# A hybrid encoder block on one core: the front stages in another order, the softmax normalised in one multiplication per token tile

## The chip, the cores and the metric

One NeuronCore of a Trainium2 chip runs the whole program: 1 launch, inputs and output in device memory. The metric is the device time of one execution in microseconds (us). The program before takes a median of 1157.8 us over three runs.

## The reference

One layer on 256 tokens of 1024 features, in float32. What is computed, cut to its lines:

```python
proj = jnp.einsum('bsd,de->bse', x, w_in[l])
(qa, ckv, qi, ki, wi, qb, kb, vb, ga, gb) = jnp.split(proj, split_at, axis=-1)
...
y_a = sparse_indexed_attention(qa, ckv, qi, ki, wi, w_uk[l], w_uv[l])
y_b = chunk_band_attention(qb, kb, vb, rel_bias[l])
merged = (jax.nn.sigmoid(ga) * (y_a @ w_branch_a[l])
          + jax.nn.sigmoid(gb) * (y_b @ w_branch_b[l]))
x = layer_norm(DN_ALPHA * x + merged @ w_out[l], ln1_g[l], ln1_b[l])
ffn = moe_ffn(x, ...)          # top 4 of 32 experts, clamped SwiGLU
x = layer_norm(DN_ALPHA * x + ffn, ln2_g[l], ln2_b[l])
```

Branch A selects 64 keys for each query with an indexer and attends to them; branch B attends to its chunk and those before it, with a bias. Both end in a softmax over keys for 8 heads.

## The kernel before, in words

The program has two parts. The **front** computes everything up to the router; the **experts** follow, 32 of them, each with 12 MB of weights.

SBUF is cut into 25 slots of 1 MB (`NSLOT`). Every weight is a chunk of one slot. SP, the queue that issues the loads, takes chunks in one fixed list (`plan`): first the front's 24 chunks (16 of `w_in`, 2 of each branch matrix, 4 of `w_out`), then the experts' chunks in the order of use. A load is issued when a slot is free; how many slots it must leave free after each chunk's use is the table `RESERVE` (`pump`). So the loads of the experts' weights begin while the front still runs, as far as its slots allow. Up to the first expert 23 of their chunks are issued.

The front's products run on exact halves. `ahead` splits chunk after chunk: ScalarE (ACT) rounds it to `hi`, in two instructions of 128x1024 (L175), and GpSimd (POOL) or VectorE (DVE) subtracts to get `lo`, again in two (L180). The table `LO_ENGINE` says which engine subtracts for each of the 24 chunks, `AHEAD` how many chunks ahead this is done.

TensorE (PE) follows the order in which the body is written. `project_T(g)` is group g of the input projections (two chunks, 96 matmuls of 256 columns, three for each pair of blocks: hi by hi, lo by hi, hi by lo; feature-major), `project(g)` the same token-major. `head_scores` makes the scores of one token tile; its sink adds scale and bias on DVE (L419). `exps` takes the maximum (DVE, L406) and then 16 exponentials per branch on ACT (L408) that also give the sums. `normalise` (L411 to L414) divides: 16 instructions per branch, one per head and token tile. `attend` turns the probabilities with 24 transposes on PE (L454), copies them to SBUF, and takes the weighted sum of the values (L464). `branch` (L511) multiplies with the branch matrix.

The order before, on PE: groups 0, 1, index scores, group 2, scores of B, group 3 (the values of B), scores of A, group 4 (gate), attend B, group 5 (gate), attend A, groups 6 and 7 (gate), branch A, branch B, output projection (`wo`), norm, router, and the first expert.

Of the kernel before, what the change touches and what calls it, by code (L numbers as in the profile page):

```python
# [48 lines left out]
def body(nc, tc, slots, sm, psp, xT_d, x_d, w_g0, w_qi, w_in, ikgb_d, wuk_d,  # L49
# [4 lines left out]
    # ---------------------------------------------------------------- slots and loads  # L54
# [42 lines left out]
    for i in range(2):  # L97
        plan(("ba", i), wba_d[i])
        plan(("bb", i), wbb_d[i])
# [27 lines left out]
    # ---------------------------------------------------------------- first loads  # L127
# [13 lines left out]
    # ---------------------------------------------------------------- constants and small loads  # L141
# [28 lines left out]
    # ---------------------------------------------------------------- exact halves of float32 operands  # L170
# [12 lines left out]
    order = [("in", i) for i in range(16)] + [("ba", 0), ("ba", 1), ("bb", 0), ("bb", 1)] + [("wo", i) for i in range(4)]  # L183
    IN, BA, BB, WO = 0, 16, 18, 20
    halves = []

    def ahead(n):
        """splits the first n chunks of that order"""
# [66 lines left out]
    def project(g, sink):  # L255
        """group g of the input projections, token-major"""
# [13 lines left out]
    def project_T(g, sink):  # L270
        """group g of the input projections, feature-major; two row blocks share a bank, so only the first starts it"""
# [21 lines left out]
    # k_idx layer norm and c_kv rms norm, token-major  # L293
# [26 lines left out]
    def head_scores(qT, kT, tb, sink):  # L320
        """pairs of heads lie on the two halves of the partitions"""
# [14 lines left out]
    # ---------------------------------------------------------------- B queries and keys, the indexer  # L336
# [51 lines left out]
    # ---------------------------------------------------------------- A queries  # L388
# [11 lines left out]
    V.memset(sB[1][0:64, :, 192:256], NEG)  # L400

# [3 lines left out]
    def exps(s, w, tb):  # L405
        V.tensor_reduce(mx[:, w, tb, :], s[tb], axis=AX.X, op=ALU.max, negate=True)  # L406
        for h in range(H):
            A.activation(s[tb][:, h, :], s[tb][:, h, :], AF.Exp, bias=mx[:, w, tb, h:h + 1],  # L408
                         accum_out=sums[:, w, tb, h:h + 1])

    def normalise(s, w, tb):  # L411
        V.reciprocal(sums[:, w, tb, :], sums[:, w, tb, :])
        for h in range(H):
            V.tensor_scalar(s[tb][:, h, :], s[tb][:, h, :], sums[:, w, tb, h:h + 1], None, op0=ALU.mult)  # L414
# [7 lines left out]
    for tb in range(NT):  # L422
        head_scores(qbT, lambda j: kbT[:, j, :], tb, score_sink(sB))
        exps(sB, 1, tb)
    free(1)
    sa0_s = slot("sa0_vb")
    sa1_s = slot("sa1")
    sA = [sa0_s[:, 0:1024].rearrange("p (h s) -> p h s", h=8), sa1_s.rearrange("p (h s) -> p h s", h=8)]
    for tb in range(NT):
        sl = slice(KOFF[tb], KOFF[tb] + KEYS[tb])  # L430
        for h in range(H):
            V.scalar_tensor_tensor(sA[tb][:, h, :], negd[:, sl], 2.0 ** -(h + 1), amask[:, sl],
                                   op0=ALU.mult, op1=ALU.add)
    free(1)
    vb = sa0_s[:, 1024:2048].rearrange("p (b c) -> p b c", b=2)
    project(3, lambda tb, p: acopy(vb[:, tb, :], p))
    normalise(sB, 1, 0)
    normalise(sB, 1, 1)
    for tb in range(NT):
        head_scores(qaT, lambda j: kaT[:, j, :], tb, score_sink(sA))  # L440
        exps(sA, 0, tb)
    free(2)

    y_s = [slot("yA"), slot("yB")]
    yHL = [[t[:, o:o + 1024].rearrange("p (j t) -> p j t", j=4) for o in (0, 1024)] for t in y_s]

    def attend(s, v, w):
        pts = [slot("pt0"), slot("pt1")]
        pT = [t[:, 0:1536].rearrange("p (b h t) -> p b h t", b=3, h=4) for t in pts]
        for j2 in range(2):  # L450
            for bi, (tb, sb) in enumerate(((0, 0), (1, 0), (1, 1))):
# [3 lines left out]
                (vcopy if bi != 1 else acopy)(pT[j2][:, bi, :, :].rearrange("p h t -> p (h t)"), p)  # L455
        for j2 in range(2):
            o = bank("pv")
            for jj in range(2):
                for tb in range(NT):
                    for sb in range(tb + 1):  # L460
                        for par in range(2):
# [3 lines left out]
                                      v[:, sb, h * 64:(h + 1) * 64], pT[j2][:, tb + sb, i, :],  # L465
                                      start=(sb == 0), stop=(sb == tb), skip_group_check=True)
            hi, lo = [t[:, 2 * j2:2 * j2 + 2, :] for t in yHL[w]]
# [3 lines left out]
    sg_s = [slot("sgA"), slot("sgB")]  # L471
    sg = [s.rearrange("p (k t) -> p k t", k=KD) for s in sg_s]

    def gate_sink(w, n):
        return lambda js, p: A.activation(sg[w][:, 4 * n + js.start:4 * n + js.stop, :], p, AF.Sigmoid)

    project_T(4, gate_sink(0, 0))
    attend(sB, vb, 1)
    free(2)
    normalise(sA, 0, 0)  # L480
    normalise(sA, 0, 1)
    project_T(5, gate_sink(0, 1))
    attend(sA, va, 0)
    free(3)
# [5 lines left out]
    mg = sg[1]  # L490
# [18 lines left out]
    yHL = [[t.bitcast(F32R) for t in hl] for hl in yHL]  # L509

    def branch(w, c, ps):  # L511
        """chunk c of a branch's rows; at the last one the gate and, for B, the sum of the two and its halves"""
        for f in range(KD):
# [10 lines left out]
            if w:  # L524
# [5 lines left out]
    for c in range(2):  # L530
        ahead(BA + c + 1 + AHEAD[BA + c])
        branch(0, c, ps)
# [5 lines left out]
    for c in range(2):  # L538
        ahead(BB + c + 1 + AHEAD[BB + c])
        branch(1, c, ps)  # L540
# [8 lines left out]
    def norm_apply(tb, groups):  # L549
        """z = (x1 - mean) * rstd, and x1 = z * g + b"""  # L550
# [38 lines left out]
    def route_sums(copy=vcopy):  # L589
        """the router's products by experts, in four sums over two row blocks each"""  # L590
# [7 lines left out]
    def route(tb):  # L598
        """the router's logits (the norm's gain in the weights, its offset in the row), and which experts a token takes"""
# [9 lines left out]
    def count_up(tb):  # L609
        """the place of each token among an expert's tokens; far off for the tokens that it doesn't take"""  # L610
# [51 lines left out]
    # the second token tile's last columns in two halves, for a shorter way from their sums to the norm  # L662
# [66 lines left out]
    # ---------------------------------------------------------------- experts  # L729
# [9 lines left out]
    def combine_weights(pt, gated):  # L739
        """pt = the gated one-hot rows turned, from their two halves of 64 columns for each token tile"""  # L740
# [6 lines left out]
    def dispatch_weights(g):  # L747
        """for the pair g of experts"""
# [39 lines left out]
    def down(hT, wd):  # L788
        """the halves of the columns on the halves of the partitions"""
# [7 lines left out]
    def rows_of(e, p, first=0, size=512):  # L797
        """an expert's rows to its half of the pair's partitions"""
# [4 lines left out]
    def combine(g):  # L803
        """adds a pair's rows to the sums"""
# [90 lines left out]
    def down_biases():  # L895
        """the gates' share of the down biases; the largest count of an expert's tokens"""
# [62 lines left out]
    # the last expert: the sums move to PSUM  # L959
# [14 lines left out]
    # ---------------------------------------------------------------- last expert's end, second norm  # L974
# [111 lines left out]
```

## Time and profile before

| | us |
|---|---|
| three runs | 1158.95, 1157.16, 1157.80 |
| median | 1157.8 |
| span of the profiled execution, first to last instruction | 1156.1 |
| first matmul of the first expert, from the span's start | 221.0 |

The profile comes from one more execution of the same program. It gives that execution's span; what lies around the span isn't in it. The lowest of the three runs is 1.1 us above the span and the median 1.7 us. Busy shares over the span: PE 92%, DVE 30%, ACT 20%, POOL 7%; the DMA engines moved 437.5 MB, 378 GB/s on average. The page's slices are 28.9 us wide; the first eight hold the front.

### The profile page before, as it was taken

The numbers are of one execution on the slowest core, as the hardware profiler recorded it, in microseconds if no ns is written. First come the engines' busy times: TensorE is split into PE (matmuls) and PEld (weight loads), VectorE is DVE, ScalarE is ACT, GpSimd is POOL, SyncE is SP. The second block draws the span as 40 slices with busy tenths as digits, with TensorE's granted clock in tenths as the row PEclk, the third lists the DMA queues.
The fourth block names the chain that finished last, engine by engine and source line by source line (L and its number), as shares of the span: only waits on it lengthen the run. The fifth ranks groups of instructions, "written<-read, shape, count | busy, mean of one in ns | idle before, by whom it ended". The sixth has DMA issues, their size and how long they took to land. (4 is left out here: it accounts for less than half of the span.)

```text
span 1156.1 us, 13824 instructions
## 1 busy us (share of the span) xinstructions
PE 1067.6 (92%) x5599; PEld 540.9 (47%) x5599; DVE 351.9 (30%) x811; ACT 227.6 (20%) x424; POOL 85.5 (7%) x60
## 2 busy tenths in 40 slices
PE   8997899999899999999899999996699999999896
PEld 8987899634244443434343434341243434343432
DVE  6797826412212322121212121210212121212124
ACT  3645342221011111111111111110011111111112
POOL 4113723000000000000000000001000000000001
PEclk9997999999899999999999999998799999999998
DMA  8940747999999999999999999999989999999995
GB/s 335 382 154 1 280 180 306 359 420 422 407 405 421 421 420 421 421 421 421 421 421 421 421 422 421 421 422 422 418 353 421 421 421 421 421 421 421 421 421 189
DMA packets 63932, 437.51 MB, mean 378 GB/s; under 512 B 7252, under 2 KB 7892, under 8 KB 11892
## 3 DMA queue, kind: packets, MB, share of 16 engines
q1 hardware_dynamic: 61270, 421.61, 88.5%
q0 software_dynamic: 1728, 12.58, 2.6%
q10 hardware_dynamic: 864, 2.36, 0.6%
q8 instruction: 46, 0.75, 0.3%
q14 instruction: 24, 0.20, 0.0%
HBM read 435.48 MB, written 1.05 MB: 378 GB/s over the span
## 5 line engine op out<-in xcount | busy, mean ns | idle before, releaser
L761 PE MATMUL gu<-ld,wa 128*64 128x512 f32 x1024 | 458.9, 602 | 27.3 <-DMA ld<-in_dram 23.4
L759 PE MATMUL gu<-ld,wa 128*64 128x512 f32 x1024 | 457.9, 601 | 7.5 <-DVEq L832 6.8
L793 PE MATMUL y<-ld,wc 128*64 128x512 f32 x992 | 240.4, 606 | 19.7 <-DMA ld<-in_dram 19.7
L759 PEld LDWEIGHTS gu<-ld,wa 128*64 128x64 f32 x1024 | 136.7, 138 | 241.0 <-issue 221.4
L780 DVE TENSOR_TENSOR wc<-tr,wb 128x256 f32<-128x256 f32 x64 | 27.0, 422 | 669.7 <-PE tr L776 669.7
L761 PEld LDWEIGHTS gu<-ld,wa 128*64 128x64 f32 x1024 | 136.2, 138 | 93.2 <-DMA ld<-in_dram 46.4
L793 PEld LDWEIGHTS y<-ld,wc 128*64 128x64 f32 x992 | 77.4, 138 | 169.6 <-issue 131.2
L175 ACT ACTIVATE wb<-gu 128x512 f32<-128x512 f32 x64 | 38.3, 598 | 442.6 <-PE gu L761 234.5
L175 ACT ACTIVATE wc<-y 64x512 f32<-64x512 f32 (+1 forms) x66 | 38.3, 580 | 239.8 <-PE y L793 234.1
L279 PE MATMUL fm<-xh,hi 128*128 128x256 f32 x224 | 66.4, 297 | 9.7 <-ACT sa_vb L175 5.4
L635 PEld LDWEIGHTS ga<-wa,x 128*128 128x128 f32 x512 | 61.6, 196 | 12.4 <-issue 12.2
L180 POOL TENSOR_TENSOR lo<-ld,hi 128x1024 fp32r<-128x1024 f32 x24 | 59.0, 2491 | 97.7 <-ACT hi L175 72.4
L279 PE MATMUL fm<-xl,hi 128*128 128x256 f32 x224 | 65.2, 291 | 0.0
L279 PE MATMUL fm<-xh,lo 128*128 128x256 f32 x224 | 65.1, 291 | 0.0
L635 PE MATMUL ga<-wa,x 128*128 128x128 f32 x512 | 64.8, 285 | 0.0
L808 PE MATMUL c<-wc,wb 128*128 128x512 f32 x120 | 54.0, 592 | 0.0
L83 POOL DMA_DIRECT2D ld<-in_dram x12 | 6.7, 558 | 608.8 <-DMA ld<-in_dram 578.1
L175 ACT ACTIVATE hi<-ld 128x1024 fp32r<-128x1024 f32 x48 | 47.1, 1048 | 17.6 <-PE fm L279 8.8
L279 PEld LDWEIGHTS fm<-xh,hi 128*128 128x128 f32 x224 | 45.0, 201 | 10.9 <-ACT sa_vb L175 5.8
L279 PEld LDWEIGHTS fm<-xl,hi 128*128 128x128 f32 x224 | 45.0, 201 | 0.2 <-issue 0.2
L279 PEld LDWEIGHTS fm<-xh,lo 128*128 128x128 f32 x224 | 44.9, 200 | 0.0
L180 DVE TENSOR_TENSOR lo<-ld,hi 128x1024 fp32r<-128x1024 f32 x24 | 33.8, 1461 | 30.2 <-ACT hi L175 27.4
(244 smaller groups left out, 882.0 us busy)
## 6 DMA issues: line engine op xcount, KB each, us to landing
ld<-in_dram SPq DMA_DIRECT2D x392, 1024.0 KB, 19.8
ld<-in_dram POOLq DMA_DIRECT2D x12, 1024.0 KB, 25.0
ld<-in_dram SPq DMA_DIRECT2D x8, 512.0 KB, 14.2
wq<-in_dram ACTq DMA_DIRECT2D x3, 512.0 KB, 8.7
biasB<-in_dram SPq DMA_DIRECT2D x1, 1024.0 KB
x<-in_dram SPq DMA_DIRECT2D x1, 1024.0 KB
g<-in_dram SPq DMA_DIRECT2D x1, 800.0 KB, 9.7
xT<-in_dram SPq DMA_DIRECT2D x3, 256.0 KB, 6.9
```

The lines of the kernel that those rows point to most:

```text
L83: eng.dma_start(part, from_)
L175: A.activation(o, i, AF.Copy)
L180: sub.tensor_tensor(lo.bitcast(F32R), t, hi, op=ALU.subtract)
L279: PE.matmul(ps[j // 2][:, j % 2 * 256:j % 2 * 256 + 256], part(i, b, k, 4)[:, j * 128:(j + 1) * 128], xHL[a][:, 4 * c + k, :], start=(c + ...
L635: PE.matmul(ps[j // per][:, (j % per) * n:(j % per + 1) * n], x1_cols(tb, j), Pt, start=(tb == 0 and j % per == 0), stop=(tb == 1), skip_g ...
L759: PE.matmul(ps[n][0:64, :], xe(j), wg(j, cs), start=(j == 0), stop=(j == KD - 1), skip_group_check=True)
L761: PE.matmul(ps[n][64:128, :], xe(j), wu(j, cs), start=(j == 0), stop=(j == KD - 1), skip_group_check=True)
L780: V.tensor_tensor(gg, pv[:, :, 0, :], bg(js), op=ALU.add)
L793: PE.matmul(p[64 * n:64 * n + 64, :], hT[:, j, :], wd(j, slice(n * 512, (n + 1) * 512)), start=(j == 0), stop=(j == KD - 1), skip_group_ch ...
L808: PE.matmul(ps[n], work["pt"][:, g % 2, tb, :], work["y"][:, n * 512:(n + 1) * 512], start=True, stop=True)
```

## The change

- The input columns are laid out in another order: groups 3 and 4 are now the gate of A, group 5 the values of B.
- The order on PE becomes: groups 0, 1, index scores, groups 2 and 3, scores of B, group 4, scores of A, group 5, turn B, group 6, weighted sum of B, group 7, turn A, first half of branch B, weighted sum of A, second half of branch B, branch A, and then `wo` as before. `attend` is cut in two for this, `turn` (the transposes) and `attend` (the weighted sum). Branch B now comes first, so the sum of the two and its halves are made in branch A.
- `normalise` is one multiplication per token tile with the reciprocal sums spread over the keys, 128x1024 and 128x2048 elements, in place of 8 per tile.
- `exps` of B moves behind group 4, `exps` of A behind group 5; the maxima are taken on their own.
- `RESERVE`, `AHEAD` and `LO_ENGINE` have other numbers. POOL now subtracts for 15 of the 24 chunks (3 to 12 without a break), DVE for 9; before it was 12 and 12.
- Comments are gone, which shifts no instruction; lines of the new program are some 10 higher.

```diff
-RESERVE = (8, 6, 5, 0, 4, 2, 5, 8, 3, 8, 1, 2, 3, 0, 8, 4, 3, 4, 1, 3, 5, 0, 0, 2, 0)
-AHEAD = (3, 4, 2, 4, 3, 3, 3, 3, 0, 0, 4, 3, 3, 4, 3, 2, 4, 3, 3, 2, 1, 4, 2, 0)
-LO_ENGINE = 'GVVGVVVVGGGGVGGGGVVGGVVV'
+RESERVE = (4, 3, 3, 3, 4, 5, 3, 3, 3, 1, 3, 3, 3, 2, 3, 1, 2, 4, 3, 1, 5, 1, 1, 1, 0)
+AHEAD = (3, 4, 3, 3, 3, 3, 3, 3, 3, 3, 3, 3, 3, 3, 3, 3, 3, 3, 3, 3, 3, 3, 2, 1, 0)
+LO_ENGINE = "GVVGGGGGGGGGGVGVGVGVGVVV"
...
-    def normalise(s, w, tb):
-        V.reciprocal(sums[:, w, tb, :], sums[:, w, tb, :])
-        for h in range(H):
-            V.tensor_scalar(s[tb][:, h, :], s[tb][:, h, :], sums[:, w, tb, h:h + 1], None, op0=ALU.mult)
+    def normalise(s, w):
+        V.reciprocal(sums[:, w], sums[:, w])
+        for tb in range(NT):
+            V.tensor_tensor(s[tb], s[tb], sums[:, w, tb, :, None].to_broadcast([128, H, KEYS[tb]]), op=ALU.mult)
...
+    project_T(3, gate_sink(0, 0))
+    for tb in range(NT):
+        head_scores(qbT, lambda j: kbT[:, j, :], tb, score_sink(sB))
+    free(1)
+    maxima(sB, 1)
...
+    project_T(4, gate_sink(0, 1))
+    exps(sB, 1)
+    for tb in range(NT):
+        head_scores(qaT, lambda j: kaT[:, j, :], tb, score_sink(sA))
     free(2)
...
+    maxima(sA, 0)
+    project(5, lambda tb, p: acopy(vb[:, tb, :], p))
+    normalise(sB, 1)
+    exps(sA, 0)
+    turn(sB, 1)
+    free(2)
     project_T(6, gate_sink(1, 0))
+    attend(vb, 1)
+    normalise(sA, 0)
     project_T(7, gate_sink(1, 1))
     free(2)
...
+    turn(sA, 0)
+    free(2)
...
     ps = [bank("br") for _ in range(4)]
     for c in range(2):
-        ahead(BA + c + 1 + AHEAD[BA + c])
-        branch(0, c, ps)
+        ahead(BB + c + 1 + AHEAD[BB + c])
+        branch(1, c, ps)
+        if c == 0:
+            attend(va, 0)
+            free(1)
...
     for c in range(2):
-        ahead(BB + c + 1 + AHEAD[BB + c])
-        branch(1, c, ps)
+        ahead(BA + c + 1 + AHEAD[BA + c])
+        branch(0, c, ps)
```

How this stands on DVE, around the normalisation of branch B. Before (`biasB` holds the scores of B, `sa` those of A, `lo` is the subtraction for a chunk):

```order
L432 SCALAR_TENSOR_TENSOR sa_836<-misc 128x256 x8
L412 RECIPROCAL sums<-sums 128x8
L414 TENSOR_SCALAR biasB_670<-biasB_670,sums 128x128 x8
L412 RECIPROCAL sums<-sums 128x8
L414 TENSOR_SCALAR biasB_671<-biasB_671,sums 128x256 x8
L419 SCALAR_TENSOR_TENSOR sa_vb<-sce,sa_vb 128x4x128
```

In the changed program, the same place:

```order
L410 TENSOR_REDUCE mx<-sa_932 128x8
L181 TENSOR_TENSOR lo<-ld,hi 128x1024 x2
L419 RECIPROCAL sums<-sums 128x16
L421 TENSOR_TENSOR biasB_660<-biasB_660,sums 128x1024
L421 TENSOR_TENSOR biasB_661<-biasB_661,sums 128x2048
L173 COPY pt_1202<-ptr 128x512 x2
```

The scores of A no longer stand behind the normalisation of B; they come ahead of it, and the subtraction for chunk 13 stands directly ahead of it now.

On ACT, around the exponentials of B. Before (`hi` is the rounding of chunks, `fm` and `tm` are a group's sums, `sgA` the gate of A, `qi` the queries of A):

```order
L175 ACTIVATE qi<-fm 128x512 x2
L408 ACT_TABLE_LOAD
L408 ACTIVATE biasB_670,sums<-biasB_670,mx 128x128 x8
L408 ACTIVATE biasB_671,sums<-biasB_671,mx 128x256 x8
L175 ACTIVATE hi<-ld 128x1024 x4
L175 ACTIVATE sa_vb<-tm 128x512 x2
L408 ACTIVATE sa_vb,sums<-sa_vb,mx 128x128 x8
```

In the changed program:

```order
L430 ACTIVATE sgA<-fm 128x512 x2
L176 ACTIVATE hi<-ld 128x1024 x4
L430 ACTIVATE sgA<-fm 128x512 x2
L415 ACT_TABLE_LOAD
L415 ACTIVATE biasB_660,sums<-biasB_660,mx 128x128 x8
L415 ACTIVATE biasB_661,sums<-biasB_661,mx 128x256 x8
L176 ACTIVATE hi<-ld 128x1024 x4
L176 ACTIVATE sa_vb<-tm 128x512 x2
```

The exponentials of B now stand behind the sigmoids of groups 3 and 4 and a table load; the four roundings behind them are those of chunks 13 and 14.

## Rows read from the trace of the kernel before

**Rows 1.** The page: GB/s of the DMA engines, by 40 slices of 28.9 us.

```profile
GB/s 335 382 154 1 280 180 306 359 420 422 407 405 421 421 420 421 421 421 421 421 421 421 421 422 421 421 422 422 418 353 421 421 421 421 421 421 421 421 421 189
```

**Rows 2.** The chain that ended last, in order of time: start us, us, what.

```profile
900.15 19.81 DMA ld<-in_dram
...
1128.29 11.35 DMA ld<-in_dram
```

**Rows 3.** Stretches: from:to, length, busy us (instructions) by engine, clock, DMA share, GB/s.

```profile
84.00:140.00 56.00, 42.46 (x350) 40.51 (x347) 47.99 (x68) 29.79 (x66) 28.20 (x12) 0.85 0.32 126
140.00:185.00 45.00, 45.00 (x378) 45.00 (x377) 14.23 (x19) 15.98 (x19) 17.32 (x12) 1.00 0.66 267
185.00:221.00 36.00, 34.88 (x269) 29.51 (x268) 24.64 (x51) 9.79 (x19) 4.15 (x3) 1.00 0.75 294
221.00:300.00 79.00, 78.95 (x381) 30.81 (x382) 19.00 (x56) 14.02 (x25) 0.00 (x0) 1.00 1.00 414
```

**Rows 4.** PE's waits from 56 to 222 us: total us, times, longest.

```profile
PE fm L279 <- ACT sa_vb L175: 5.4, 1, 5.4
PE fm L279 <- DVE sa_vb L419: 4.2, 1, 4.2
PE ptr L454 <- DVE sa L414: 1.9, 1, 1.9
PE pv L464 <- DVE pt L172: 1.9, 1, 1.9
```

**Rows 5.** Stretches around those waits, columns as in rows 3.

```profile
90.04:94.10 4.06, 4.06 (x19) 4.06 (x20) 4.06 (x3) 0.43 (x1) 4.06 (x3) 0.50 0.01 4
...
99.20:104.20 5.00, 5.00 (x23) 5.00 (x24) 4.93 (x7) 3.17 (x16) 0.00 (x0) 0.50 0.00 0
110.20:112.97 2.77, 2.77 (x28) 2.60 (x28) 1.96 (x3) 2.76 (x5) 0.00 (x0) 1.00 0.00 0
...
129.82:139.04 9.22, 7.28 (x69) 6.50 (x69) 7.74 (x15) 3.09 (x4) 4.67 (x2) 0.81 0.44 166
139.04:162.34 23.30, 23.30 (x196) 23.30 (x195) 4.44 (x7) 5.82 (x7) 5.86 (x7) 1.00 0.62 251
```

**Rows 6.** PE by line: count, ns min/median/max, first and last start us.

```profile
L264 PE MATMUL tm<-hi,xh x16: 389/389/499, 70.6 to 80.9; 128*128 128x512 f32 x16
L330 PE MATMUL sce<-kidxT_ckvT,qi x16: 272/374/378, 81.7 to 84.2; 64*128 64x128 f32 x8, 64*128 64x256 f32 x8
```

**Rows 7.** ACT in order of time: start us, us, instruction, [idle before <- releaser].

```profile
77.28 1.28 ACT L408 ACT_TABLE_LOAD   x1 [8.78 <-DVE mx L406]
78.57 0.41 ACT L408 ACTIVATE biasB<-biasB,mx 128x128 f32<-128x128 f32 x1
...
85.62 3.89 ACT L175 ACTIVATE hi<-ld 128x1024 fp32r<-128x1024 f32 x4
89.41 1.06 ACT L175 ACTIVATE sa_vb<-tm 128x512 f32<-128x512 f32 x2
```

**Rows 8.** DVE and POOL in order of time, 81 to 99 us.

```profile
86.06 10.14 DVE L414 TENSOR_SCALAR biasB<-biasB,sums 128x128 f32<-128x128 f32 x8
86.80 9.33 POOL L180 TENSOR_TENSOR lo<-ld,hi 128x1024 fp32r<-128x1024 f32 x4 [18.86 <-ACT hi L175]
...
96.36 2.19 DVE L414 TENSOR_SCALAR biasB<-biasB,sums 128x256 f32<-128x256 f32 x8
```

**Rows 9.** The subtractions L180, 20.5 to 25.5 us and then 26 to 30 us, columns of rows 6.

```profile
L180 POOL TENSOR_TENSOR lo<-ld,hi x2: 2412/2891/3370, 19.3 to 21.6; 128x1024 fp32r<-128x1024 f32 x2
L180 DVE TENSOR_TENSOR lo<-ld,hi x2: 2210/2802/3393, 20.6 to 22.7; 128x1024 fp32r<-128x1024 f32 x2
...
L180 DVE TENSOR_TENSOR lo<-ld,hi x3: 1211/1212/3393, 22.7 to 27.1; 128x1024 fp32r<-128x1024 f32 x3
```

**Rows 10.** DVE by line, the other instructions of the chain that moves.

```profile
L406 DVE TENSOR_REDUCE mx<-biasB x2: 1220/1753/2286, 75.7 to 79.3; 128x8 f32<-128x1024 f32 x1, 128x8 f32<-128x2048 f32 x1
...
L432 DVE SCALAR_TENSOR_TENSOR sa_vb<-misc x8: 282/285/289, 81.5 to 82.9; 128x128 f32<-128x128 f32 x8
```

More of the change, by code (lines that the diff above doesn't have):

```diff
@@ L97, in body @@
     for i in range(2):
+        plan(("bb", i), wbb_d[i])
+    for i in range(2):
         plan(("ba", i), wba_d[i])
-        plan(("bb", i), wbb_d[i])
     for i in range(4):
@@ L180, in split @@
         sub.tensor_tensor(lo.bitcast(F32R), t, hi, op=ALU.subtract)
-    order = [("in", i) for i in range(16)] + [("ba", 0), ("ba", 1), ("bb", 0), ("bb", 1)] + [("wo", i) for i in range(4)]
-    IN, BA, BB, WO = 0, 16, 18, 20
+    order = [("in", i) for i in range(16)] + [("bb", 0), ("bb", 1), ("ba", 0), ("ba", 1)] + [("wo", i) for i in range(4)]
+    IN, BB, BA, WO = 0, 16, 18, 20
     halves = []
@@ L420, in score_sink, with gate_sink, turn @@
         return sink
[L422 to L449, printed above, removed]
+    def gate_sink(w, n):
+        return lambda js, p: A.activation(sg[w][:, 4 * n + js.start:4 * n + js.stop, :], p, AF.Sigmoid)
+    y_s = [None, None]
+    yHL = [None, None]
+    pts = [None, None]
+    def turn(s, w):
+        pts[w] = [slot("pt0"), slot("pt1")]
         for j2 in range(2):
+            pT = pts[w][j2][:, 0:1536].rearrange("p (b h t) -> p b h t", b=3, h=4)
             for bi, (tb, sb) in enumerate(((0, 0), (1, 0), (1, 1))):
@@ L454, in attend @@
                     PE.transpose(p[:, i * 128:(i + 1) * 128], s[tb][:, 4 * j2 + i, sb * 128:(sb + 1) * 128], ident)
-                (vcopy if bi != 1 else acopy)(pT[j2][:, bi, :, :].rearrange("p h t -> p (h t)"), p)
+                (vcopy if bi != 1 else acopy)(pT[:, bi, :, :].rearrange("p h t -> p (h t)"), p)
+    def attend(v, w):
+        y_s[w] = slot("y")
+        halves_of = [y_s[w][:, o:o + 1024].rearrange("p (j t) -> p j t", j=4) for o in (0, 1024)]
+        yHL[w] = [t.bitcast(F32R) for t in halves_of]
         for j2 in range(2):
+            pT = pts[w][j2][:, 0:1536].rearrange("p (b h t) -> p b h t", b=3, h=4)
             o = bank("pv")
@@ L464, in attend @@
                             PE.matmul(o[64 * par:64 * par + 64, jj * 256 + tb * 128:jj * 256 + (tb + 1) * 128],
-                                      v[:, sb, h * 64:(h + 1) * 64], pT[j2][:, tb + sb, i, :],
+                                      v[:, sb, h * 64:(h + 1) * 64], pT[:, tb + sb, i, :],
                                       start=(sb == 0), stop=(sb == tb), skip_group_check=True)
-            hi, lo = [t[:, 2 * j2:2 * j2 + 2, :] for t in yHL[w]]
+            hi, lo = [t[:, 2 * j2:2 * j2 + 2, :] for t in halves_of]
             split(o.rearrange("p (j t) -> p j t", j=2), hi, lo, vcopy, V)
         free(2)
[L471 to L478, printed above, removed]
-    free(2)
[L480 to L484, printed above, removed]
+    project_T(3, gate_sink(0, 0))
+    for tb in range(NT):
+        head_scores(qbT, lambda j: kbT[:, j, :], tb, score_sink(sB))
+    free(1)
+    maxima(sB, 1)
+    sa0_s = slot("sa0_vb")
+    sa1_s = slot("sa1")
+    sA = [sa0_s[:, 0:1024].rearrange("p (h s) -> p h s", h=8), sa1_s.rearrange("p (h s) -> p h s", h=8)]
+    vb = sa0_s[:, 1024:2048].rearrange("p (b c) -> p b c", b=2)
+    for tb in range(NT):
+        sl = slice(KOFF[tb], KOFF[tb] + KEYS[tb])
+        for h in range(H):
+            V.scalar_tensor_tensor(sA[tb][:, h, :], negd[:, sl], 2.0 ** -(h + 1), amask[:, sl],
+                                   op0=ALU.mult, op1=ALU.add)
+    free(1)
+    project_T(4, gate_sink(0, 1))
+    exps(sB, 1)
+    for tb in range(NT):
+        head_scores(qaT, lambda j: kaT[:, j, :], tb, score_sink(sA))
+    free(2)
+    maxima(sA, 0)
[4 more added lines that the diff above has]
+    free(2)
     project_T(6, gate_sink(1, 0))
+    attend(vb, 1)
+    normalise(sA, 0)
     project_T(7, gate_sink(1, 1))
     free(2)
-    mg = sg[1]
+    turn(sA, 0)
+    free(2)
+    mg = sg[0]
     ones = sm.tile([1, 128], F32, name="ones")
@@ L507, in body @@
            allow_small_or_imprecise_dtypes=True)
-    yHL = [[t.bitcast(F32R) for t in hl] for hl in yHL]
     def branch(w, c, ps):
@@ L530, in body @@
     for c in range(2):
-        ahead(BA + c + 1 + AHEAD[BA + c])
-        branch(0, c, ps)
+        ahead(BB + c + 1 + AHEAD[BB + c])
+        branch(1, c, ps)
+        if c == 0:
+            attend(va, 0)
+            free(1)
     free()
@@ L1053 @@
         w[:, :, ranges(2)].transpose(1, 0, 2),
-        chunks(ranges(5, 6, 0, 7, 8, 9)),
+        chunks(ranges(5, 6, 0, 8, 7, 9)),
         np.stack([np.tile(a["idx_k_norm_g"][0], 2), np.tile(a["idx_k_norm_b"][0], 2), a["kv_norm_g"][0]], axis=1),
```

15 lines of the change are left out of this document (9 added, 6 removed).

## The prediction

> **What bounds the kernel now.** I read the page's slices first: from the ninth slice (231 us) on the DMA engines move some 421 GB/s in nearly every slice, two dips apart [rows 1]. Then the chain of waits: from 900 us it goes from load to load, ten loads of experts' weights in a row and, behind the last sums, an eleventh [rows 2]. So the expert part runs at the speed of its loads, and the change doesn't touch it. What the change can move is when that stream starts to flow without a break. The stretches show that: the DMA share is 0.32, 0.66 and 0.75 in the three stretches of the front and 1.00 from 221 us, when the first expert begins [rows 3]. The reason is slots: the front holds them, and loads wait until its chunks are used. Both programs issue 23 chunks of the experts before the first expert's first product, and from the output projection on the loads wait for the same instructions in the same order. The front's DMA idle time is 0.68 x 56 + 0.34 x 45 + 0.25 x 36 = 62 us [rows 3], far more than any saving here. Hence: each us by which the first expert begins earlier is a us off the end.
>
> The front itself is bound by PE from 56 us on. PE is busy all 45.00 us from 140 to 185, but only 42.46 of 56 from 84 to 140 [rows 3]. Its waits there are four: 5.4, 4.2, 1.9 and 1.9 us, together 13.4 [rows 4]. The first is for the values of B, the other three for DVE. Behind them the clock is low: 0.50 (the level of 1.2 GHz) for 4.06 us after the first and for 5.00 us after the second, and 0.81 on average over 9.22 us around the last two [rows 5]. That loses 2.0 + 2.5 + 0.19 x 9.22 = 6.3 us of work. Without waits and at the full level the first expert would begin at 221.0 - 13.4 - 6.3 = 201.3 us. This is the floor of the change.
>
> Why DVE was late: eight normalising instructions of 128x128 took 10.14 us, eight of 128x256 only 2.19 [rows 8]. POOL was subtracting from 86.80 to 96.13 in four instructions of 2.33 us. So some small DVE instructions sat out a whole POOL instruction each.
>
> **The change, part by part.** The walk below uses durations of the old rows and times of the new kernel from its start.
>
> PE's work is the same in another order; only waits can change. Up to 55.8 us nothing moves. A feature-major group takes 23.30 / 2 = 11.65 us [rows 5], scores 2.9, the token-major group 11.1 [rows 6], the transposes 2.8 [rows 5]. Group 2 then ends at 67.8 us, group 3 at 79.4, scores of B at 82.3, group 4 at 93.95, scores of A at 96.85, group 5 at 107.95. Turn B wants its normalised scores there.
>
> Halves for these groups: POOL has chunks 3 to 12 now, 2.4 us a half [rows 9]. Chunk 3 is subtracted before group 1 uses it. Even if POOL began chunk 4 only at 55.8 us, chunk 9 would be done twelve halves later, at 84.6, and is wanted at 88. Chunk 12 can be rounded only when group 4 has used chunk 8 and freed its slot, at 88; its halves are done near 94 and wanted at 110.7. So I cost POOL's longer list at nothing; the cover is 3 us at chunk 9 and 16 at chunk 12, and without it each us would be PE's.
>
> ACT: the exponentials of B stand behind the second sigmoid of group 4. Group 4 ends at 93.95, the sigmoid takes some 0.6 (two evictions of that size took 1.06), the table load 1.28, the 16 exponentials 85.62 - 78.57 = 7.05 [rows 7]. They end at 102.9. Before, they ended at 85.6: the change moves them 17 us down, behind PE work that was already there. The four roundings of chunks 13 and 14 follow, 0.97 us each [rows 7], to 106.8. ACT loads its table once more than before (1.28 us); that falls between rounding and the sigmoid of group 6, whose gate nobody wants until the branches.
>
> DVE: the scores of B are taken at 80 to 84, the maxima end at 87.6 (1.22 + 2.29), the 16 mask instructions follow (1.7 + 2.8) [rows 10]. Two of these may sit out POOL's halves of chunk 12, so the scores of A and their maxima end near 104. Nobody on PE waits for them. The subtraction for chunk 13 can start at 103.9, when its first half is rounded, and ends at 106.3. Then come the reciprocal (0.2) and the two multiplications. A multiplication of 128x1024 with both inputs in SBUF takes 1.21 us when alone [rows 9]. For 128x2048 no row exists: the maximum over 2048 elements took 2.29 [rows 10], twice 1.21 is 2.42, eight narrow ones took 2.19; I take 2.3, between 2.2 and 2.4.
>
> Does POOL hold these up too? Rows 9 say yes, and in turn: a DVE subtraction begun while POOL ran took 2.21 and 3.39 in place of 1.21, and POOL's second took 3.37 in place of 2.41. Each waits for the other's instruction to end. In the new order POOL's two halves of chunk 14 start at 106.3, just ahead of the multiplications. So: POOL to 108.7, tile 0 to 109.9, POOL to 112.2, tile 1 to 114.5. The bounds for this wait are 0 and two POOL instructions, 4.8 us; the walk gives 4.4, and I take it, since every row with such an overlap shows it.
>
> By instructions alone the merged form isn't cheaper. The Trainium skill (VectorE: DVE Perf Modes, Why `tensor_tensor` can't do 2×_2P or 4×) says that a two-source operation cannot use both read ports for one tensor, as the one-source multiplication by a scalar can; by that the 3072 elements of a branch would cost 3.2 us instead of 1.6 at 0.96 GHz, 1.6 us more (an estimate from that page), and the forecast would be 1.6 us later if the old form had no fixed cost. The rows have that fixed cost in them: 2.19 for eight of 256 columns, against my 2.3. The gain of the merged form is that it can meet POOL twice, not sixteen times.
>
> PE then: it does the four transposes of tile 0 by 110.4 or waits, and has tile 1 at 114.5, where 110.7 was the end of turn B on the floor. With 0.5 us done it idles 5.9 us in all. After a gap of 5.4 us the clock was at 0.50 for 4.06 us, after 4.2 us for 5.00 [rows 5]: 2.0 to 2.5 us lost, I take 2.3. **The new wait costs 8.2 us.** Group 6 starts near 118.9.
>
> After that: the weighted sum of B at 130.6 finds its transposes copied (the last ACT copy stands behind the exponentials of A, from 108.7, done near 116, and is done by 119.6). The normalisation of A (135 to 139) is hidden by group 7, which ends at 145, when turn A wants it; without that cover it would cost its 3.8 us. Weighted sum A stands behind the first half of branch B, 5.8 us (a quarter of 23.30) that cover its copies. The later chunks alternate between POOL, 4.8 us each, and DVE, 2.4, against 5.8 us of products for each. From branch A on the order is the old one.
>
> Loads: the first chunk of an expert waits for POOL's half of chunk 16, some 129.5 us, before it was issued near 139. In the last 60 us the new order frees as many slots as the old, one of them somewhat earlier. I cost it at nothing; it is covered by the DMA idle time above.
>
> **The sum.** 201.3 + 8.2 = 209.5 us for the first expert, 11.5 earlier than 221.0. The span goes from 1156.1 to 1144.6. The span lies 1.7 below the median of the runs, and I keep that: **1146.3 us**.
>
> **Rivals.** (1) The multiplications slip in ahead of POOL. They and POOL's halves become ready within 0.4 us of each other. The Trainium skill (SBUF — State Buffer, Who interferes with whom) lets whichever begins first keep the shared port for its whole instruction. Rows 9 agree: 1.21 alone, 3.39 behind POOL. Then tile 1 is ready at 106.5 + 1.2 + 2.3 = 110.0, PE idles 1.6 us and loses some 0.8 to the clock (half of the 1.75 of the last two gaps [rows 5]): 203.7 us, 17.3 earlier, 1140.5. For it: a shift of 0.4 us is enough. Against: both of POOL's halves must lose the race.
>
> (2) The mask instructions meet more of POOL. If ACT rounds chunk 12 late or DVE is late, four POOL halves stand over the 16 mask instructions instead of two; the scores of A, the maxima and the subtraction for chunk 13 are some 4 us later, and with them turn B: 213.5 us, 1150.3. Against it: the subtraction waits for ACT until 103.9 anyway, so the first us of this are free.
>
> (3) Slower: the clock stays low. If short gaps follow turn B, groups 6 and 7 (23.30 us [rows 5]) run at 1.2 GHz and take 23.3 more: 232.8, 1169.6. It decides at the restart: PE must find a new gap within the 4 to 5 us in which the clock is still at 0.50. Against it: before, the second gap fell right there, and after it 5.00 us were enough to be at 1.00 again by 110.20 [rows 5].
>
> (4) No change: the loads don't follow. If the stream up to the first expert had no room, the end would stay at 1157.8. Against it: the 62 us of idle DMA time.
>
> **How the numbers follow.** Forecast 0.63, (1) 0.18, (2) 0.11, (3) 0.04, (4) 0.04. A measurement of this kernel tells about 0.2% (2.3 us) from no change. The forecast, (1) and (2) are all faster by more: 0.92; same 0.04; slower 0.04. The forecast's own spread is from the bounds: the lock's wait 0 to 4.8 and the clock 2.0 to 2.5 on one side, a few us of small waits not seen on the other. The range goes from just under (1) to just over (2): 1139.8 to 1151.5; (3) and (4) and a little of (2) are left out.
>
> **What would show it.** Right: PE's only long wait before the first expert is the one of turn B's transposes for DVE, near 6 us, with the clock at 0.50 behind it; the multiplication of 128x2048 shows near 4.6 us beside a POOL subtraction; the first expert's products start near 209.5; the GB/s of the expert slices are unchanged. Wrong: a wait of PE for POOL's `lo` (POOL became the bound), a wait at turn A, or a stream of loads with gaps after the first expert.

## The result, and the profile after

| us | before | changed |
|---|---|---|
| median of the runs compared | 1157.84 (4 runs, 1157.16 to 1158.95) | 1147.12 (4 runs, 1146.5 to 1147.6) |
| span of the profiled execution | 1156.1 | 1144.8 |
| first matmul of the first expert | 221.0 | 210.3 |

The ratio is 0.9906, with a 95% interval of 0.9892 to 0.992: faster, by 10.7 us. The forecast was 1146.3 us, in a range from 1139.8 to 1151.5.

The page's GB/s row (40 slices, now 28.6 us wide) of the changed kernel, to be held against [rows 1]:

```profile
GB/s 323 408 93 203 150 275 288 401 422 421 410 410 421 422 421 421 421 421 421 422 421 421 421 421 421 421 421 421 404 367 421 422 421 421 420 421 421 421 420 186
```

The plateau is the same 421; in the eighth slice, ahead of it, stand 401 where 359 stood. The chain that ended last, in order of time (start us, us, what), has the loads of [rows 2] 11.3 and 11.4 us earlier:

```profile
888.88 19.89 DMA ld<-in_dram
...
1116.91 11.40 DMA ld<-in_dram
```

The stretches of [rows 3] (from:to, length, busy us and instructions of PE, PEld, DVE, ACT, POOL, then clock, DMA share, GB/s):

```profile
84.00:140.00 56.00, 50.14 (x385) 46.82 (x384) 38.09 (x48) 32.82 (x86) 21.06 (x8) 0.94 0.51 192
140.00:185.00 45.00, 45.00 (x367) 43.13 (x366) 27.15 (x35) 18.14 (x21) 14.29 (x11) 1.00 0.76 286
```

From 84 to 140 us PE is busy for 50.14 us where it was 42.46, at a mean clock of 0.94 in place of 0.85. Of the four waits of [rows 4] none is left. PE's waits from 56 to 212 us (total us, times, longest):

```profile
PE ptr L444 <- DVE biasB L421: 5.9, 2, 3.7
PE cum L626 <- DVE selb L620: 0.4, 1, 0.4
```

The one long wait is that of turn B's transposes for the two multiplications. DVE there, in order of time (start us, us, instruction, [idle before <- releaser]):

```profile
88.87 1.69 DVE L479 SCALAR_TENSOR_TENSOR sa_vb<-misc 128x128 f32<-128x128 f32 x8
90.48 2.76 DVE L479 SCALAR_TENSOR_TENSOR sa<-misc 128x256 f32<-128x256 f32 x8
...
104.80 2.36 DVE L181 TENSOR_TENSOR lo<-ld,hi 128x1024 fp32r<-128x1024 f32 x2 [2.00 <-issue]
107.08 0.25 DVE L419 RECIPROCAL sums<-sums 128x16 f32<-128x16 f32 x1
107.36 7.47 DVE L421 TENSOR_TENSOR biasB<-biasB,sums 128x1024 f32<-128x1024 f32 x2
```

and POOL beside it, with the first half of chunk 12 and both halves of chunk 14:

```profile
90.03 5.46 POOL L181 TENSOR_TENSOR lo<-ld,hi 128x1024 fp32r<-128x1024 f32 x1 [3.48 <-ACT hi L176]
106.74 5.95 POOL L181 TENSOR_TENSOR lo<-ld,hi 128x1024 fp32r<-128x1024 f32 x2 [8.92 <-ACT hi L176]
```

The multiplication's line by forms (ns min/median/max, first and last start us) gives the price of the company. Branch B had POOL beside it, branch A had not:

```profile
L421 DVE TENSOR_TENSOR biasB<-biasB,sums x2: 3121/3776/4431, 107.4 to 110.4; 128x1024 f32<-128x1024 f32 x1, 128x2048 f32<-128x2048 f32 x1
L421 DVE TENSOR_TENSOR sa_vb<-sa_vb,sums x1: 1224/1224/1224, 136.0 to 136.0; 128x1024 f32<-128x1024 f32 x1
L421 DVE TENSOR_TENSOR sa<-sa,sums x1: 2285/2285/2285, 137.2 to 137.2; 128x2048 f32<-128x2048 f32 x1
```

Last the stretches behind the wait (columns as above): the last twenty transposes of turn B, and group 6.

```profile
115.09:119.59 4.50, 4.50 (x21) 4.50 (x22) 1.73 (x3) 2.48 (x9) 0.00 (x0) 0.50 0.12 25
119.24:131.58 12.34, 12.34 (x100) 12.21 (x100) 3.05 (x3) 5.86 (x7) 4.76 (x2) 0.95 0.44 167
```

The clock is at its lower level, 1.2 GHz, for the 4.50 us behind the wait, and back at 2.4 GHz within group 6.

### The profile page after: what moved, and what is told of

Same layout as the page of the kernel before. It is cut to its first block, busy times and chain, and to the rows that moved or that the text cites. A ratio compares the mean times of both kernels' runs of the same rounds, so it can differ in the third digit from the quotient of the medians.

```text
span 1144.8 us, 13796 instructions
## 1 busy us (share of the span) xinstructions
PE 1061.5 (93%) x5599; PEld 534.7 (47%) x5599; DVE 333.1 (29%) x775; ACT 228.6 (20%) x425; POOL 103.6 (9%) x66
## 3 DMA queue, kind: packets, MB, share of 16 engines
q10 hardware_dynamic: 864, 2.36, 0.6%
## 5 line engine op out<-in xcount | busy, mean ns | idle before, releaser
L181 POOL TENSOR_TENSOR lo<-ld,hi 128x1024 fp32r<-128x1024 f32 x30 | 76.8, 2594 | 62.7 <-ACT hi L176 49.1
L795 ACT ACTIVATE wa<-wc 128x256 f32<-128x256 f32 x64 | 26.6, 416 | 76.4 <-DVE wc L794 76.4
```

The costliest lines, as they stand in the source:

```text
L795: A.activation(sg_, gg, AF.Sigmoid, scale=1.702)
```

## The experiments

For each trace I cut the span in three: the **beginning**, up to the first matmul of group 2 of the projections; the **middle**, from there to the first expert's first matmul; the **rest**, to the end. All is in us; "wait for bd" is explained at the fourth experiment. The ratios are to the kernel before, run on the same chip.

| kernel | beginning | middle | rest | wait for bd | median | ratio, 95% interval |
|---|---|---|---|---|---|---|
| before | 55.79 | 165.21 | 935.09 | 3.4 | 1157.84 | |
| changed | 56.57 | 153.73 | 934.50 | 2.7 | 1147.12 | 0.9906 [0.9892, 0.992] |
| 1 merged form alone | 55.53 | 155.07 | 936.61 | 4.2 | 1149.32 | 0.9929 [0.9916, 0.9943] |
| 2 order and tables alone | 56.02 | 152.43 | 934.84 | 2.9 | 1145.15 | 0.9895 [0.988, 0.991] |
| 3 multiplications first | 55.30 | 144.89 | 935.14 | 3.0 | 1137.56 | 0.9834 [0.9818, 0.985] |
| 4 wait filled | 55.95 | 151.13 | 938.39 | 5.3 | 1146.06 | 0.9903 [0.989, 0.9917] |
| 5 bias products later | 55.39 | 153.85 | 933.68 | none | 1144.61 | 0.9886 [0.9871, 0.9902] |
| 6 both 3 and 5 | 56.28 | 144.90 | 933.57 | none | 1136.74 | 0.9819 [0.9805, 0.9832] |
| 7 chunk 14 on DVE | 55.91 | 150.84 | 935.66 | 3.9 | 1144.70 | 0.9889 [0.9874, 0.9904] |
| 8 both 4 and 5 | 57.29 | 151.16 | 933.81 | none | 1145.39 | 0.9893 [0.9878, 0.9908] |
| 9 changed again | 56.07 | 153.03 | 936.38 | 3.8 | 1146.39 | 0.9907 [0.989, 0.9923] |
| 10 number 8 again | 57.05 | 151.16 | 935.73 | none | 1143.31 | 0.988 [0.9863, 0.9896] |

The kernel before ran beside the experiments; its medians were 1157.28 (beside 1 to 4), 1157.96 (5 to 8) and 1157.00 (9 and 10).

**1 and 2: which part carries the gain.** The first takes the kernel before and merges the multiplications.

```diff
-        for h in range(H):
-            V.tensor_scalar(s[tb][:, h, :], s[tb][:, h, :], sums[:, w, tb, h:h + 1], None, op0=ALU.mult)
+        V.tensor_tensor(s[tb], s[tb], sums[:, w, tb, :, None].to_broadcast([128, H, KEYS[tb]]), op=ALU.mult)
```

The second takes the changed kernel and puts the sixteen narrow ones back.

```diff
-        V.reciprocal(sums[:, w], sums[:, w])
         for tb in range(NT):
-            V.tensor_tensor(s[tb], s[tb], sums[:, w, tb, :, None].to_broadcast([128, H, KEYS[tb]]), op=ALU.mult)
+            V.reciprocal(sums[:, w, tb, :], sums[:, w, tb, :])
+            for h in range(H):
+                V.tensor_scalar(s[tb][:, h, :], s[tb][:, h, :], sums[:, w, tb, h:h + 1], None, op0=ALU.mult)
```

> The kernel before, with one thing of the change: the softmax is normalised by one multiplication per token tile (128x1024, 128x2048) in place of eight. The order of the stages, the engines of the subtractions and the tables stay. Theory A (the merged form carries most of the gain, since the sixteen narrow instructions sat out one POOL subtraction after another): of PE's four waits the second (4.2 us, with 2.5 us of clock behind it) and the two of 1.9 us nearly vanish, the first (5.4 us, for the values of B) stays; the first expert's first product near 212 us instead of 221.0, the time near 1148.8 us (1146 to 1151.5). Theory B (the order of the stages carries the gain; the merged form still waits for POOL, twice, for 4.4 us): the second wait is only shortened by 1 to 2 us, the first product is at 219 us or later, the time 1155.5 to 1158.

> The changed kernel, with the sixteen narrow multiplications per branch (one per head and token tile) put back; order and tables are those of the change. Theory A (in the new order only two POOL subtractions stand beside the normalisation of B, and both forms meet both): within 1 us of the changed kernel, 1146.2 to 1148.2 us, first product of the first expert near 210.7 us. Theory B (each narrow instruction still sits out a POOL instruction, so the merged form is needed in the new order as well): the normalisation of B takes 10 us and more, the wait of PE at the turn of B grows from 5.9 to 10 us or more, 1152 to 1157 us. If B comes out together with theory B of the run before, order and merged form need each other.

Theory A held in both by its cause; number 2 came out 1.1 us below its range (1145.15, expected 1146.2 to 1148.2). The merged form alone took 8.0 us off (1157.28 to 1149.32), the rest of the change alone 12.1, both together 10.7. They don't add: each removes the same waits. Number 2 holds the new order and the new tables (`RESERVE`, `AHEAD`, `LO_ENGINE`) together; these two weren't tried apart, and it is `LO_ENGINE` that gives chunk 13 to DVE. With the merged form alone, PE's waits from 56 us on (total us, times, longest) begin with

```profile
PE fm L279 <- ACT sa_vb L175: 5.4, 1, 5.4
PE pv L463 <- DVE pt L172: 2.9, 2, 2.2
```

The first wait of [rows 4] stands as it was, 4.2 and 1.9 are gone, and the wait for `pt` has grown from 1.9 to 2.9. In the changed kernel the narrow instructions cost no more than the merged ones. DVE in the second experiment, in order of time:

```profile
106.77 5.66 DVE L422 TENSOR_SCALAR biasB<-biasB,sums 128x128 f32<-128x128 f32 x8
...
112.57 2.19 DVE L422 TENSOR_SCALAR biasB<-biasB,sums 128x256 f32<-128x256 f32 x8
```

The eight small ones took 5.66 us in place of the 10.14 of [rows 8], because two of POOL's subtractions stood beside them instead of four: two of the eight took 2.17 and 2.38 us and the other six 0.28, where before four took 2.38 to 2.42. All sixteen took about as long as the two merged ones (8.0 us from 106.77, against 7.5), but PE needn't wait for all of them. Its transposes in the second experiment, in order of time:

```profile
109.04 0.30 PE L445 MATMUL ptr<-ident,biasB 128*128 128x128 f32 x1 [0.99 <-PE tm L265]
111.30 0.72 PE L445 MATMUL ptr<-ident,biasB 128*128 128x128 f32 x3 [1.96 <-DVE biasB L422]
113.03 4.63 PE L445 MATMUL ptr<-ident,biasB 128*128 128x128 f32 x20 [1.00 <-PE ptr L445]
```

The last twenty start at 113.03, while DVE is still at the second tile (112.57 to 114.76): a transpose needs one head. The merged instruction gives all heads at once, at 114.84, so there they start at 115.09. The middle is 1.3 us shorter with the narrow form than in the first trace of the changed kernel, 0.6 than in its second (9); the medians (ratios 0.9895 and 0.9906, intervals that overlap) can't tell the two apart.

**3: the multiplications ahead of the subtraction for chunk 13.**

```diff
-    project(5, lambda tb, p: acopy(vb[:, tb, :], p))
     normalise(sB, 1)
+    project(5, lambda tb, p: acopy(vb[:, tb, :], p))
     exps(sA, 0)
```

> The changed kernel, with the two multiplications for branch B written ahead of the subtraction for chunk 13 on DVE, so that they begin near 103.9 us, before POOL's subtraction for chunk 14 (106.7 us). Theory A (the place behind that subtraction and beside POOL is what made them late): the two take 1.2 and 2.4 us and end near 107.6, before PE wants them; the wait of 5.9 us at the turn of B and the 2.3 us of clock behind it vanish, the first expert's first product is near 202.2 us, the time near 1139 us (1137.5 to 1141.5). Theory B (a wait that takes its place: the subtraction for chunk 13, which the sixth group wants from about 113 us, or POOL's for chunk 14 comes late by as much): 1143 us or more, with a wait of PE for lo in the sixth group. Theory C (the loads set the end, not the first expert's begin): 1146 to 1148 us though the first product is earlier.

Theory A, and the largest effect of the study: 1137.56 us. DVE in this kernel, in order of time:

```profile
102.82 3.43 DVE L421 TENSOR_TENSOR biasB<-biasB,sums 128x1024 f32<-128x1024 f32 x2
106.16 6.75 DVE L181 TENSOR_TENSOR lo<-ld,hi 128x1024 fp32r<-128x1024 f32 x2
```

The two multiplications take 3.43 us instead of 7.47. Now it is the subtraction for chunk 13 that meets POOL: 6.75 us in place of 2.36. Nobody waits for it; group 6 wants that chunk later. PE has no wait before the router, and the first stretch of [rows 3] is full in this kernel (columns as above):

```profile
84.00:140.00 56.00, 56.00 (x461) 53.15 (x460) 42.09 (x54) 38.13 (x93) 26.42 (x14) 1.00 0.58 219
```

The middle is 8.84 us shorter than in the changed kernel. That is the price of its one wait (8.1 us by the changed kernel's second trace, number 9).

**4: PE's wait filled with products that nobody reads.**

```diff
+                if w and j2 == 0 and bi == 0:
+                    warm(54)
                 (vcopy if bi != 1 else acopy)(pT[:, bi, :, :].rearrange("p h t -> p (h t)"), p)
...
+    warm(30)
     turn(sB, 1)
```

> The changed kernel with products of a zero tile that nobody reads put into PE's wait at the turn of B: 30 ahead of the turn, 54 behind its first four transposes, so that PE has work while it waits. The wait for DVE stays as it is. Theory A (the wait costs its 5.9 us and beyond that 2.3 us of work at the lower clock): the granted clock stays near 1.00 through the turn, its last twenty transposes take 2.3 us instead of 4.5, the first expert's first product is near 207.7 us, the time near 1144.5 us. Theory B (the lower clock behind the wait costs nothing that counts, or the added products delay the transposes by as much as they save): 1146.6 to 1148 us.

In this kernel's stretches behind the wait the clock is 1.00, and the transposes and group 6 take 2.38 and 11.75 us instead of 4.50 and 12.34:

```profile
114.49:116.87 2.38, 2.38 (x22) 2.38 (x23) 1.62 (x3) 1.97 (x8) 0.00 (x0) 1.00 0.00 0
116.62:128.37 11.75, 11.75 (x101) 11.62 (x101) 3.32 (x4) 6.17 (x7) 4.77 (x2) 1.00 0.67 242
```

The middle is 2.6 us shorter, as theory A has it. But the median fell by 1.1 us only, and in the trace the rest took 938.39 us instead of 934.50. (The traced execution took 1147.17 us, 1.1 above the median of its kernel, so not all of that is in the median.) I had counted on the rest not changing, so this was a miss, and it led to the next experiment. The trace shows where the rest grew. Behind the fourth expert's gate and up products PE waits for `bd`, the experts' output biases, a load of 128 KB that takes 15.8 us here to land among the weights' loads. PE's wait (total us, times, longest):

```profile
PE bd L924 <- DMA bd<-in_dram: 5.3, 1, 5.3
```

Two stretches of the same kernel behind that wait:

```profile
300.00:310.00 10.00, 10.00 (x34) 2.97 (x34) 1.75 (x7) 0.00 (x0) 0.00 (x0) 0.67 1.01 414
310.00:320.00 10.00, 10.00 (x68) 6.50 (x66) 3.99 (x12) 3.48 (x7) 0.00 (x0) 1.00 0.76 307
```

First the clock is low (0.67), then the DMA share falls to 0.76: PE has been late with its slots, and the stream of loads stops for a while. In this trace no load is issued from 293.1 us until PE's next down product releases one at 304.8 us, 97.7 us after the first expert's first product; in the changed kernel that came after 94.8. The changed kernel waits 2.7 us there and keeps a share of 0.99 in the second of these stretches.

**5 and 6: the bias products behind the down product of the third expert**, in the changed kernel and in that of experiment 3. The load is issued where it was; `products` holds the rest of `down_biases`.

```diff
         if e == 3:
-            ov_s = down_biases()
+            ov_s, products = down_biases()
         if e >= 1:
             run_down(e - 1)
+            if e == 3:
+                products()
```

> The changed kernel; in the fourth expert the products with the experts' output biases (eight of 32x512, whose 128 KB load takes 13.2 us in the crowd of the other loads) stand behind the third expert's down product instead of ahead of it; the load is issued where it was. So far the time from the first expert's first product to the end went with PE's wait for that load: 934.5 us for a wait of 2.7 (the changed kernel), 934.8 for 2.9, 935.1 for 3.0 and 3.4, 936.6 for 4.2, 938.4 for 5.3. Theory A (the wait and the lower clock behind it make slots free late, and the stream of loads stalls once): the wait vanishes, that time falls to 932 to 933.5 us, the first product stays near 210.3, the time is 1144.5 to 1146.2 us. Theory B (the wait only goes along with another cause, the loads set the pace): 934.5 us again, 1147 us.

> The version with the two multiplications ahead of the subtraction for chunk 13, and the bias products moved as in the run before. Its first expert's first product was at 200.2 us and the time from there 935.1 us with a wait of 3.0 for the biases. Theory A (both effects add): 200.2 + 932.5 + 1.7, near 1134.5 us (1133.5 to 1136). Theory B (the wait for the biases is not a cause): 1137 to 1138 us.

PE's wait for the load is gone. What is left there in number 5 is a wait for ACT's copy (PE's waits, 222 to 340 us):

```profile
PE bd L923 <- ACT bd L176: 1.4, 1, 1.4
```

The stretch in which number 4 had a DMA share of 0.76, in number 5:

```profile
310.00:320.00 10.00, 10.00 (x56) 5.37 (x57) 4.30 (x12) 2.30 (x5) 0.00 (x0) 0.96 1.01 420
```

The rest is 933.68 and 933.57 us, 0.8 and 1.6 below the kernels that they came from: theory A by its cause, with less of a gain than expected (the rest was to fall to 932 to 933.5 us). The medians are 1144.61 (expected 1144.5 to 1146.2) and 1136.74 (expected 1133.5 to 1136, so that missed by a little). By its ratio number 6 is the fastest kernel here, 1.8% below before, though its interval overlaps that of number 3.

**7: POOL taken away from the multiplications.** Chunk 14 is subtracted by DVE.

```diff
-LO_ENGINE = "GVVGGGGGGGGGGVGVGVGVGVVV"
+LO_ENGINE = "GVVGGGGGGGGGGVVVGVGVGVVV"
```

> The changed kernel with chunk 14 subtracted by DVE in place of POOL, ahead of the multiplications, so that POOL runs nothing beside them; DVE has 2.4 us more to do before them. Theory A (it is POOL's two subtractions that stretch the multiplications from 1.2 and 2.3 to 3.1 and 4.4 us): they take 1.2 and 2.3 us, begin some 2.4 us later and end near 113.4 instead of 114.84; the first product of the first expert is some 1.5 us earlier than 210.3, the time near 1145.6 us (1144.8 to 1146.5). Theory B (the multiplication with the spread reciprocals is slow by itself): they take 3.1 and 4.4 us again, 2.4 us later, and the time is near 1149.5 us.

DVE in this kernel, in order of time:

```profile
104.14 4.63 DVE L181 TENSOR_TENSOR lo<-ld,hi 128x1024 fp32r<-128x1024 f32 x4 [2.00 <-issue]
108.69 0.24 DVE L419 RECIPROCAL sums<-sums 128x16 f32<-128x16 f32 x1
108.96 3.42 DVE L421 TENSOR_TENSOR biasB<-biasB,sums 128x1024 f32<-128x1024 f32 x2
```

Theory A. With 2.3 us more to do, DVE is done earlier, at 112.4 instead of 114.8 (0.7 of that is the earlier beginning), since nothing stretches the multiplications (3.42 us). The wait is 4.1 us instead of 5.9, and the middle 2.9 us shorter, where 1.5 was expected: the clock recovered sooner too, the transposes took 3.88 us and group 6 11.75. The time, 1144.70 us, is just below the range expected (1144.8 to 1146.5).

**8, 9 and 10: does what is won in the middle reach the end?** Number 8 joins the edits of 4 and 5, 9 is the changed kernel and 10 is number 8 again.

> The kernel with the added products of a zero tile in PE's wait at the turn of B, and the bias products moved as in the first run of this group. Without that move its first product was 3.2 us earlier than the changed kernel's, but the time only 1.1 us shorter; its wait for the biases was 5.3 us and the time behind the first product 938.4. Theory A (the gain of the clock was lost at the biases): the time behind the first product falls to 932 to 934 us, 1141 to 1143 us in all. Theory B (what was won at the turn of B doesn't reach the end for another reason, as the loads don't come earlier): 1144.5 us or more.

> The changed kernel itself once more, beside the next run, to tell which part of the time varies from execution to execution. From the eight traces of the changed order so far: the second group began between 55.3 and 57.3 us, from there to the first expert's first product it took 153.73 and 153.85 us in the two kernels with the same front, and the rest 933.6 to 938.4 us with the wait for the biases. Theory A (the front from the second group on is fixed; the beginning and the wait for the biases vary): 153.7 to 153.9 us for that part again, with another beginning; the time 1145.5 to 1148 us. Theory B (the wait at the turn of B varies, since DVE and POOL race there): that part differs by 1 us or more.

> The kernel with the added products at the turn of B and the bias products moved, once more on the same chip as the run before. Its part from the second group to the first expert's first product was 151.16 us, 2.6 less than in the changed kernel, and its rest 933.81 us, 0.7 less, and yet its median was only 1.7 us below the changed kernel's, from another chip and another call. Theory A (both gains reach the end, the medians of different calls differ by more than 1 us): 151.0 to 151.3 us and 933.5 to 934 us again, the median 2.5 to 4.5 us below that of the run before. Theory B (something before or behind them gives them back): the median 0.5 to 2 us below, and the trace shows one of the two parts longer.

Number 8 is a miss by the time, 1145.39 us, which is theory B; its trace speaks for theory A (a middle of 151.16, a rest of 933.81) but for the late beginning, 57.29. Side by side on one chip, number 10 was 3.1 us below number 9, with the same middle of 151.16 to the hundredth: theory A, but for the rest, which was to be 933.5 to 934 us again. Its profiled execution was the slowest of its four (1145.64, the others 1142.47 to 1143.93), and its rest of 935.73 has a longer halt of the loads near 830 us: a DMA share of 0.72 where number 8, the same kernel, has 0.82, which makes 2.0 us over 20, and the two rests differ by 1.9. That stretch in number 10:

```profile
820.00:840.00 20.00, 16.80 (x77) 6.71 (x75) 0.00 (x0) 1.19 (x2) 0.00 (x0) 0.99 0.72 288
```

The same stretch in the changed kernel's first trace:

```profile
820.00:840.00 20.00, 16.93 (x76) 5.87 (x74) 0.00 (x0) 1.19 (x2) 0.00 (x0) 0.99 0.79 320
```

Why that halt varies wasn't tried. The middle of number 9, 153.03 us, fits neither of its theories (153.7 to 153.9, or 1 us and more away). The wait at turn B is the same 5.9 us to the tenth, and DVE ends the multiplications 58.3 us after group 2 begins in both traces and in number 5, so nothing shows DVE and POOL racing there from run to run. (PE's wait in number 5 is 5.4 us, since its first four transposes ran at a clock of 0.50 and took 1.08 us instead of 0.63.) What differs by 0.7 us is the clock behind the wait; in number 9 the two stretches behind the wait are

```profile
114.60:118.88 4.28, 4.28 (x22) 4.28 (x23) 1.73 (x3) 2.26 (x9) 0.00 (x0) 0.54 0.17 21
118.64:130.39 11.75, 11.75 (x101) 11.62 (x101) 3.05 (x3) 5.97 (x7) 4.76 (x2) 1.00 0.45 173
```

## Why the prediction was right

**The walk.** The trace begins its group 2 0.8 us later than the walk did, and everything behind is later by about that much:

| step | forecast | trace, less 0.8 us |
|---|---|---|
| group 3 ends | 79.4 | 79.4 |
| exponentials of B end | 102.9 | 102.9 |
| subtraction for chunk 13 | 103.9 to 106.3 | 104.0 to 106.4 |
| group 5 ends | 107.95 | 107.8 |
| tile 0 normalised | 109.9 | 109.7 |
| tile 1 normalised | 114.5 | 114.0 |
| group 6 begins | 118.9 | 118.4 |
| first expert | 209.5 | 209.5 |

**The floor.** The forecast was 201.3 us, that is 145.5 for the middle. Experiment 3, which has no long wait, measured 144.89 and experiment 6 144.90, 0.6 us less.

**The one new wait.** Forecast 5.9 us of idling and 2.3 of clock. (By the walk's own times the idling is 114.5 - 107.95 - 0.5 = 6.05 us, so the 5.9 is a slip of 0.15.) The trace has 5.9 of idling. Taking the clock alone back gave 2.6 us (the changed kernel against experiment 4) and 1.9 (9 against 10), taking the whole wait away 8.8 (8.1 by number 9), where 8.2 was forecast. In the first trace the floor is 0.6 us lower and the wait 0.6 dearer than forecast, so it is in part luck that its middle, 153.73, is the forecast's 153.7; in number 9 it is 153.03. The cause is shown from two sides: with POOL's work taken away the multiplications need 3.42 us instead of 7.47 (7), and so they do when they come ahead of it (3). Forecast were 4.6 us for the larger one; it took 4.43.

**The lock.** The rows show that a two-input DVE instruction and a POOL subtraction wait for each other's end: 1.22 and 2.29 us alone, 3.12 and 4.43 beside POOL. The Trainium skill (SBUF — State Buffer, Who interferes with whom) has the rule: the second to be issued blocks until the first is done, when DVE takes two inputs from SBUF and POOL reads there as well. The trace agrees for the multiplications, and for the subtraction in experiment 3 (6.75 us for two halves, 2.36 alone).

**What the change's gain is made of.** Here the prediction's words were too simple. It named the merged form's gain ("it can meet POOL twice, not sixteen times") as a part of the sum. Experiments 1 and 2 show that this is so in the old order, with the old tables, only. In the new one the narrow form also meets POOL twice, and it lets PE start on single heads. The sum didn't suffer, since it was built from the floor and one wait, but a reader would have taken from it that the merged form is needed. It isn't: the new order and tables do as well without it. Which of those two carries the gain stays open.

**The mask instructions** were to sit out two of POOL's halves. They didn't: the sixteen ran from 88.87 to 93.24 in 4.4 us, their old durations. It was POOL that waited, 5.46 us for a half that takes 2.4 alone. No term hung on this, because DVE's next job waited for ACT anyway: ACT begins the roundings of chunk 13 at 103.67 us, behind the exponentials, and DVE, idle for 2.00 us by then, starts at 104.80.

**The loads.** Forecast was that a us at the first expert is a us at the end, with a rest of 1144.6 - 209.5 = 935.1 us. From before to the changed kernel the first expert moved by 10.7 us and the end by 11.3. Over all traces the middle ranged from 144.89 to 165.21 us and the rest only from 933.6 to 938.4, so the step holds. What it lacked is the wait for `bd`: in the kernels that have it, the rest grows, if not evenly, from 934.50 to 938.39 as the wait grows from 2.7 to 5.3 us, and with the wait removed it is 933.6 to 933.8 in three traces of four.

**The rivals.** (1), the multiplications ahead of POOL, didn't happen; written so, it is experiment 3, and worth more than the 5.8 us that the rival gave, since no wait was left at all. (2), masks that meet more of POOL: no, see above. (3), the clock stays low: group 6 ran at 0.95 and group 7 at 1.00. (4), loads that don't follow: no.

## What to carry to other kernels

Build the forecast from a floor (the bound engine without waits, at full clock) and price each wait that the new order makes, with the clock behind it: here that came out within 1 us. Where two engines share a port, write the instruction that someone waits for ahead of the one that nobody waits for: one line moved gave nearly as much again as the whole change. Two cures for the same wait don't add, so try each alone before keeping both.

## What was not expected

- Who waits at the shared port isn't always the same. Short narrow multiplications let POOL in between them and took 10.14 us for eight [rows 8]. The run of sixteen mask instructions didn't: POOL's half lasted 5.46 us and ended 2.25 us after the last of them. The runs don't show what makes the difference.
- From group 2 to the first expert, traces of kernels with the same middle agree to 0.1 us where no wait drops the clock (151.13, 151.16 and 151.16; 144.89 and 144.90). With the clock's drop they differ by 0.8 (153.03 to 153.85). Over all traces the beginning ranged from 55.3 to 57.3 us and the rest, where PE doesn't wait for `bd`, from 933.6 to 935.7. The two traces of the kernel of 8 and 10 have the latest beginnings (57.29 and 57.05), though number 4 has the same program up to there and 55.95; the cause stays open. The median of four runs moved by 2.1 us for that kernel from one group of runs to another (1145.39 and 1143.31), so stretches of a trace told more here than medians.
- A load of 128 KB among loads of 1 MB took 13.2 us to land in the changed kernel, and PE waited 2.7 to 5.3 us for it in the traces that have the wait. By the rests, that cost 2.7 to 4.6 us in number 4 (938.39 against 933.81 and 935.73 without the wait); by the medians, 0.7 to 2.8 (1146.06 against 1145.39 and 1143.31).
